# Attention stage of a hybrid trunk: two lanes of blocks become three, the lane table gets other numbers, and TensorE follows program order there

## The chip, the cores and the metric

The program runs on one core of a Trainium2 chip. The metric is the device time of one execution in microseconds. Three executions of the kernel before took 3175.34, 3176.96 and 3179.81 us; the median is 3176.96 us.

## The reference

Two layers of an encoder trunk over 1024 positions of width 1024, in float32. Layer 0 mixes with a recurrent part; layer 1, where the change is, mixes with chunked softmax attention over 16 heads of 64. Cut to what matters:

```python
def chunk_band_attention(h, w_qkv, q_g, k_g, rel_bias):
    qkv = (h @ w_qkv).reshape(bsz, seq, 3, C_HEADS, C_HEAD_DIM)
    q = rmsnorm(qkv[:, :, 0], q_g) * (C_HEAD_DIM ** -0.5)
    k = rmsnorm(qkv[:, :, 1], k_g)
    v = qkv[:, :, 2]
    ...
    bias = rel_bias[:, jnp.clip(rel, -C_MAX_REL, C_MAX_REL) + C_MAX_REL]
    def one_chunk(c):                       # 64 queries, own chunk and the 8 before
        s = jnp.einsum('bqhd,bkhd->bhqk', q_c, k_b) + bias
        prob = jax.nn.softmax(jnp.where(valid, s, -jnp.inf), -1)
        return jnp.einsum('bhqk,bkhd->bqhd', prob, v_b)
```

After it come the output projection, a squared-ReLU MLP and a gated embedding, as in layer 0.

## The kernel before

The attention part of layer 1 is written as generators ("lanes") that a small planner, `run` (L128), steps through. The planner has a clock of its own, `now`. Each product that a lane emits adds its estimated TensorE time. When a lane yields a name, it may go on only once the number under that name in the table `LAT` has passed; when it yields a tuple such as `("at", 3)`, it sleeps until another lane marks that tuple. Among the lanes that may go on, the first in the list is taken. So the table and the list decide the order in which instructions are written.

Work is cut into 16 steps `s`: head pair `pr` and half `hf` of the sequence. Three kinds of lane run:

- `attn_ins` (last in the list) makes queries, keys and values of a step. Each step has four chunks of 128 rows, and a chunk is 24 matmuls of 384 columns into a bank named `dps` (two banks). ScalarE and VectorE read each chunk out (L1742, L1746, L1747), GpSimd squares the result in two halves (`sq`, L1754), and VectorE sums and normalises. This lane may be three steps ahead of the attention, no more (`("at", s - 3)`). After step 15 it goes on with dense products of the tail (`dps<-act,wq`, 512 columns).
- `attn_norms` transposes the queries and keys of a step on TensorE (`dps<-ident,qk`) and splits them into a high and a low part (`F`, `Ql`).
- `attn_lane` (two of them before) takes the next of 64 blocks: a step, one of its two heads, and two row tiles of 128 queries. For each of the two tiles a block computes the near scores into `sn` (two banks), adds the bias `toep` and takes the maximum on VectorE (L1838); computes the far scores, where there are any, into `sf` (one bank; L1845 to L1848 read it); and takes exponentials, sum and scale on ScalarE and VectorE (L1848 to L1855) in a tile `pb`. Then it transposes `pb` on TensorE into `pt` (two banks, L190), splits that into `ptile` on ScalarE and VectorE (L347, L348), and multiplies with the values into `po` (one bank). Half 1 of a pair has far scores in all its tiles, half 0 only in its last one.

The names that the planner looks up in a block are `attn_block0` (after each tile's scores), `attn_block1` (between the scores and the transposes), `attn_block2` (after each bank of transposes) and `attn_block3` (before the product with the values).

What is written is not what an engine runs. The framework schedules each engine's queue anew by its own timeline model, so before the change TensorE's order in this stage is the framework's, not the lanes'. Each engine then runs its queue strictly in that order, waiting on semaphores.

Of the kernel before, what the change touches and what calls it, by code (L numbers as in the profile page):

```python
# [17 lines left out]
P = 128  # L18
# [3 lines left out]
HB = 512  # L22
NT = T // P
C = 128
NEG = -1.0e30
# [54 lines left out]
    "gdn_back2": 0.48,  # L80
    "gdn_back3": 1.30,
    "gdn_back4": 1.83,
    "attn_norm0": 0.24,
    "attn_block0": 0.97,
    "attn_block1": 4.45,
    "attn_block2": 0.43,
    "attn_block3": 0.94,
    "qk": 11.25,
    "norm": 1.28,
    "end_front": 46.33,  # L90
    "end_mid": 0.83,
    "end_back": 1.12,
# [15 lines left out]
class Trunk:  # L108
# [1510 lines left out]
    def layer1_in(self):  # L1619
        nc, tc, a = self.nc, self.tc, self.a  # L1620
        with ExitStack() as es:
            self.psm = es.enter_context(self.pool("psml1", space=PSUM))
            wp = self.wp = es.enter_context(self.pool("l1a", 2))
            self.wr = es.enter_context(self.pool("l1wr", 2))
            self.w1 = es.enter_context(self.pool("l1w1"))
            l1 = es.enter_context(self.pool("l1", 2))
            self.sm = es.enter_context(self.pool("sml1", 2))
            self.yd = [[self.dr.tile([P, HB], F32, tag=f"yd{k}{hf}", name="yd") for hf in range(2)] for k in range(NK)]
            rbl = l1.tile([P, 16], F32, tag="rbl", name="rbl", bufs=1)
            nc.sync.dma_start(out=rbl, in_=a["rb_last"].rearrange("(o c) -> o c", o=1).broadcast_to((P, 16)))  # L1630
# [45 lines left out]
    def attn_norms(self, steps, l1):  # L1676
# [11 lines left out]
    def attn_lane(self, steps, jobs, l1, rbl):  # L1688

        for s, h, b in jobs:  # L1690
            yield ("in", s)
            yield from self.attn_block(s, *steps[s], h, b, l1, rbl)

    def weights3(self, odd):

# [89 lines left out]
            st[nm] = F  # L1785
            yield "attn_norm0"

    def attn_block(self, s, pr, hf, h, blk, l1, rbl):

        nc, psm, sm = self.nc, self.psm, self.sm  # L1790
        V, A, G = nc.vector, nc.scalar, nc.gpsimd
        st = self.st[s]
        m0 = 4 * hf + 2 * blk
        if hf == 0 and blk == 0:
            t = st["toep"][h]
            G.tensor_scalar(t, t, rbl[:, 2 * pr + h:2 * pr + h + 1], None, op0=ALU.subtract)
# [31 lines left out]
        for m in (m0, m0 + 1):  # L1828
            n0 = max(0, m - 2)
            nn = m - n0 + 1  # L1830
            f0 = max(0, m - 4)
            nf = n0 - f0
            pn = psm.tile([P, HB], F32, tag="sn", name="sn", bufs=2)
            score(pn[:, 0:nn * P], m, n0, nn)
            mx = sm.tile([P, 4], F32, tag="mx", name="mx", bufs=4)
            pb = self.wp.tile([P, 5 * P], F32, tag="pb", name="pb", bufs=4)
            S = pb[:, nf * P:(nf + nn) * P]
            V.tensor_tensor_reduce(S, pn[:, 0:nn * P], toep[:, (3 - nn) * P:], op0=ALU.add, op1=ALU.max,  # L1838
                                   scale=1.0, scalar=NEG, accum_out=mx[:, 0:1])
            l = sm.tile([P, 4], F32, tag="l", name="l", bufs=4)  # L1840
            if nf:
                pf = psm.tile([P, HB], F32, tag="sf", name="sf")
                score(pf[:, 0:nf * P], m, f0, nf)
                if m >= 4:
                    V.memset(pf[64:128, 0:64], NEG)  # L1845
                V.reduce_max(mx[:, 1:2], pf[:, 0:nf * P], axis=AX.X)
                V.tensor_scalar(mx[:, 2:3], mx[:, 0:1], mx[:, 1:2], -1.0, op0=ALU.max, op1=ALU.mult)
                A.activation(pb[:, 0:nf * P], pf[:, 0:nf * P], AF.Exp, bias=mx[:, 2:3], accum_out=l[:, 1:2])  # L1848
            else:
                V.tensor_scalar(mx[:, 2:3], mx[:, 0:1], -1.0, None, op0=ALU.mult)  # L1850
            A.activation(S, S, AF.Exp, bias=mx[:, 2:3], accum_out=l[:, 0:1])
            if nf:
                V.tensor_tensor(l[:, 0:1], l[:, 0:1], l[:, 1:2], op=ALU.add)
            V.reciprocal(l[:, 2:3], l[:, 0:1])
            A.activation(pb[:, 0:(nf + nn) * P], pb[:, 0:(nf + nn) * P], AF.Copy, scale=l[:, 2:3])  # L1855
            probs.append((pb, f0))
            yield "attn_block0"
# [9 lines left out]
        for b in range(bank + 1):  # L1867
            pt = psm.tile([P, HB], F32, tag="pt", name="pt", bufs=2)
            for j, (bb, o, c0, c1) in place.items():
                if bb != b:  # L1870
                    continue
                for e in range(2):
                    if c0 <= 128 * e < c1:
                        pb, f0 = probs[e]
                        self.tr(pt[:, o + 128 * e - c0:o + 128 * e - c0 + P],
                                            pb[:, (j - f0) * P:(j - f0 + 1) * P], self.ident)
            t = self.wp.tile([P, 2, HB], F32R, tag="ptile", name="ptile", bufs=3)
            self.split_scaled(t, pt[:, 0:used[b]], None, slice(0, used[b]))
            pts.append(t)
            yield "attn_block2"  # L1880
# [3 lines left out]
        for j, c0, c1 in segs:  # L1884
            b, o, _, _ = place[j]
# [112 lines left out]
```

## Time and profile before

| what | value |
|---|---|
| median of three runs | 3176.96 us |
| the profiled execution, its own time | 3175.69 us |
| span of the profiled execution | 3174.0 us |
| mean granted TensorE clock over the span | 0.973 |
| first dense product of the attention stage starts | 1751.1 us |
| first scores start | 1789.4 us |
| last product with the values ends | about 2371 us |

The profile counts time from the first instruction. Rows of a listing in order of time begin with start and duration; rows of groups give line, engine, operation, output and inputs, count, then busy time and mean duration, then the time that the engine sat idle just before these instructions and what ended that wait. "PE" is TensorE's matrix array, "PEld" its weight load, DVE is VectorE, ACT is ScalarE, POOL is GpSimd, SPq the queue that issues most transfers. A matmul's recorded duration includes its run through the array, and the next may start before it ends, so a matmul's duration is longer than the distance between two starts. The attention stage is the stretch from 1751 to 2371 us. Layer 0 lies before it; the dense products of the tail lie behind it.

### The profile page before, as it was taken

The page shows a single profiled execution, that of the slowest core. Times are in us where ns is not written, and L with a number is a line of the kernel's source. Part 1 is how long each engine was busy: PE and PEld are TensorE (multiplying, and loading weights), DVE is VectorE, ACT ScalarE, POOL GpSimd, SP SyncE. Part 2 cuts the span into 40 slices and gives each one's busy share as a digit, 9 for nine tenths or more (in the row PEclk, how much of TensorE's full clock was granted, in tenths as well). Part 3 has the DMA queues.
Part 4 walks back from the last instruction along what each step waited for, and adds up shares of the span by engine and source line. Part 5 has one row for each costly group of instructions (what it writes and reads, how often), then busy time and mean ns, then how long its engine had stood idle before and what let it go on. Part 6 is the DMA issues. An engine that isn't in the chain of part 4 may idle for free.

```text
span 3174.0 us, 46034 instructions
## 1 busy us (share of the span) xinstructions
PE 3057.5 (96%) x17576; PEld 2523.9 (80%) x17576; DVE 2018.1 (64%) x4020; ACT 1387.8 (44%) x2640; POOL 536.1 (17%) x978
## 2 busy tenths in 40 slices
PE   7999999999999999999999989999999999999999
PEld 5777777777778888888887888888788888888887
DVE  6546666567849666655556576776769666655552
ACT  4323433333427554311223577777757555312221
POOL 6524443444500000000005111110200000000002
PEclk8989999999999999999999999999999999999999
DMA  3212112112345333522213100110255332522213
GB/s 128 77 48 64 50 43 85 54 57 64 126 153 209 136 120 112 190 93 100 99 54 129 58 32 33 47 39 16 76 197 205 136 120 107 199 93 93 107 47 106
DMA packets 144716, 309.60 MB, mean 98 GB/s; under 512 B 40944, under 2 KB 43120, under 8 KB 144496
## 3 DMA queue, kind: packets, MB, share of 16 engines
q1 hardware_dynamic: 126064, 273.10, 25.1%
q10 hardware_dynamic: 18432, 33.56, 2.7%
q8 instruction: 138, 2.26, 0.3%
q14 instruction: 82, 0.67, 0.1%
HBM read 232.16 MB, written 74.45 MB: 97 GB/s over the span
## 4 chain that ended last, share of the span: by engine, by line
PE 79%; DVE 10%; ACT 4%; DMA 4%; issue 2%; POOL 1%; SPq 0%; DVEq 0%; POOLq 0%; ACTq 0%
PE dps L175 67%; PE ch L175 2%; PE po L175 1%; PE pm L175 1%; PE iz L175 1%; PE tp L175 1%; DVE ptile L348 1%; PE pt L190 1%; DVE f L1056 1%; DMA wraw<-in_w_out 1%; PE sn L175 1%; DMA wraw<-in_w_qkv 1%; DVE wlo L302 1%; DVE pb L1838 1%; POOL subt L413 1%
## 5 line engine op out<-in xcount | busy, mean ns | idle before, releaser
L175 PE MATMUL dps<-r,act 128*128 128x512 f32 x3528 | 824.4, 392 | 0.0
L175 PEld LDWEIGHTS dps<-r,act 128*128 128x128 f32 x3528 | 662.2, 188 | 145.6
L175 PE MATMUL dps<-xg,whi 128*128 128x512 f32 x1280 | 437.9, 423 | 16.2 <-ACT xg L350 7.1
L175 PE MATMUL dps<-late,act 128*128 128x512 f32 x1536 | 352.9, 391 | 0.0
L175 PEld LDWEIGHTS dps<-late,act 128*128 128x128 f32 x1536 | 288.5, 188 | 63.1
L1495 POOL TENSOR_TENSOR pn<-pn,prs 128x512 f32<-128x512 f32 x32 | 47.1, 1475 | 1621.3 <-ACT prs L384 1527.3
L175 PE MATMUL dps<-wq,act 128*128 128x384 f32 x1536 | 304.8, 343 | 8.0 <-DVE vs L1747 4.2
L175 PEld LDWEIGHTS dps<-xg,whi 128*128 128x128 f32 x1280 | 237.2, 197 | 67.0 <-ACT xg L350 7.1
L175 PEld LDWEIGHTS dps<-wq,act 128*128 128x128 f32 x1536 | 264.5, 190 | 12.6 <-DVE vs L1747 7.0
L175 PE MATMUL dps<-xg,wlo 128*128 128x512 f32 x640 | 260.4, 408 | 2.0 <-DVE wlo L302 2.0
L1371 DVE TENSOR_TENSOR late<-late,dps 128x512 f32<-128x512 f32 x224 | 152.7, 684 | 152.4 <-PE dps L175 120.3
L1470 DVE TENSOR_TENSOR xw<-xw,dps 128x512 f32<-128x512 f32 x192 | 131.5, 685 | 154.6 <-PE dps L175 151.4
L1269 ACT CAST act<-act 128x1024 fp32r<-128x1024 f32 (+1 forms) x99 | 94.7, 963 | 282.9 <-DMA act<-in_w 119.4
L1269 ACT CAST act<-late 128x512 fp32r<-128x512 f32 x210 | 124.5, 618 | 139.5 <-PE dps L175 120.2
L1270 DVE TENSOR_TENSOR act<-late,act 128x512 fp32r<-128x512 f32 x210 | 139.7, 686 | 25.9 <-ACT act L1269 25.7
L175 PEld LDWEIGHTS dps<-xg,wlo 128*128 128x128 f32 x640 | 125.5, 196 | 33.2 <-DVE wlo L302 4.1
L301 ACT CAST whi<-wraw 128x1024 fp32r<-128x1024 f32 x78 | 81.7, 1048 | 152.7 <-PE dps L175 91.4
L175 PE MATMUL dps<-xw,act 128*128 128x512 f32 x576 | 138.9, 392 | 0.0
L175 PEld LDWEIGHTS dps<-xw,act 128*128 128x128 f32 x576 | 108.1, 188 | 24.1
L1270 DVE TENSOR_TENSOR act<-act 128x1024 fp32r<-128x1024 f32 (+1 forms) x99 | 109.9, 1114 | 18.3 <-ACT act L1269 17.2
L175 PE MATMUL po<-ptile,vs 128*128 128x256 f32 (+1 forms) x576 | 103.3, 293 | 17.5 <-DVE ptile L348 8.5
L302 DVE TENSOR_TENSOR wlo<-wraw,whi 128x1024 fp32r<-128x1024 f32 x78 | 99.3, 1274 | 27.5 <-ACT whi L301 27.1
(472 smaller groups left out, 5284.9 us busy)
## 6 DMA issues: line engine op xcount, KB each, us to landing
act<-in_w SPq DMA_DIRECT2D x68, 512.0 KB
hd<-late ACTq DMA_DIRECT2D x128, 256.0 KB
late<-in_w SPq DMA_DIRECT2D x60, 512.0 KB
wraw<-in_w_in SPq DMA_DIRECT2D x56, 512.0 KB
act<-hd SPq DMA_DIRECT2D x56, 512.0 KB
wraw<-in_w_out SPq DMA_DIRECT2D x21, 512.0 KB
wraw<-in_w_qkv SPq DMA_DIRECT2D x21, 512.0 KB
pn<-pnd SPq DMA_DIRECT2D x32, 256.0 KB
```

Of the source, the lines that this page charges most:

```text
L175: return self.begin(self.nc.tensor.matmul(out, lhsT, rhs, start=start, stop=stop))
L190: return self.begin(self.nc.tensor.transpose(out, in_, ident))
L301: nc.scalar.copy(hi, raw)
L302: nc.vector.tensor_tensor(lo, raw, hi.bitcast(F32), op=ALU.subtract)
L348: nc.vector.tensor_tensor(dst[:, 1, sl], src, dst[:, 0, sl].bitcast(F32), op=ALU.subtract)
L413: E.tensor_tensor(o, X[:, 0:i, i:i + 1].broadcast_to((NP, i, n)), Bq[:, i:i + 1, i + 1:16].broadcast_to((NP, i, n)), op=ALU.mult)
L1056: V.scalar_tensor_tensor(y, raws[j][:, i:i + HB], cw(i), y, op0=ALU.mult, op1=ALU.add)
L1269: A.copy(hi, s)
L1270: V.tensor_tensor(lo, s, hi.bitcast(F32), op=ALU.subtract)
L1371: V.tensor_tensor(r, t, u, op=ALU.add)
L1470: V.tensor_tensor(x[n][:, sl], x[n][:, sl], ps, op=ALU.add)
L1495: G.tensor_tensor(pn, pn, prs[:, sl], op=ALU.mult)
```

## The change

Three things change in this stage, and nothing elsewhere.

1. Seven numbers of the table `LAT` become larger. The planner's waits inside a block and before a step's scores grow with them.
2. Three `attn_lane` generators run where two did. Two tiles get more buffers to match: `pb` 6 for 4, `ptile` 4 for 3. The banks `sn`, `sf`, `pt`, `po` and `dps` stay as many as they were.
3. The lanes run inside a context that keeps TensorE in program order; the other engines are scheduled by the framework as before.

The subtraction that prepares the bias tile (two GpSimd instructions per head) also moves: from the first block of each head into `attn_norms`, for both heads at once.

```diff
-    "attn_block0": 0.97,
-    "attn_block1": 4.45,
+    "attn_block0": 1.80,
+    "attn_block1": 7.00,
...
-            self.run([self.attn_lane(steps, jobs, l1, rbl) for _ in range(2)] + [self.attn_norms(steps, l1), self.attn_ins(steps, l1)])
+
+            with tc.manual_schedule(engines={mybir.EngineType.PE}):
+                self.run([self.attn_lane(steps, jobs, l1) for _ in range(3)] + [self.attn_norms(steps, l1, rbl), self.attn_ins(steps, l1)])
...
+            for h in range(0 if hf else 2):
+                t = self.st[s]["toep"][h]
+                self.nc.gpsimd.tensor_scalar(t, t, rbl[:, s + h:s + h + 1], None, op0=ALU.subtract)
+                self.nc.gpsimd.memset(t[0:64, 320:384], NEG)
...
-        if hf == 0 and blk == 0:
-            t = st["toep"][h]
-            G.tensor_scalar(t, t, rbl[:, 2 * pr + h:2 * pr + h + 1], None, op0=ALU.subtract)
-            G.memset(t[0:64, 320:384], NEG)
...
-            pb = self.wp.tile([P, 5 * P], F32, tag="pb", name="pb", bufs=4)
+            pb = self.wp.tile([P, 5 * P], F32, tag="pb", name="pb", bufs=6)
...
-            t = self.wp.tile([P, 2, HB], F32R, tag="ptile", name="ptile", bufs=3)
+            t = self.wp.tile([P, 2, HB], F32R, tag="ptile", name="ptile", bufs=4)
```

TensorE runs the same instructions in both kernels. How they stand differs over the whole stage; three places follow. A row is one or more instructions next to each other in an engine's queue, with line, operation, output and inputs, shape, count, and in brackets the engines whose semaphores the first of them waits for.

**First place, TensorE, the far scores of step 3** (second half of the second head pair). Before, ahead of the step's second group of far scores (`sf`):

```order
L175 MATMUL po<-ptile,vs 128x256 [waits Activation_49]
L175 MATMUL po<-ptile,vs 128x256 [waits DVE_49]
L175 MATMUL po<-ptile,vs 128x128 x2
L175 MATMUL dps<-wq_16732,act 128x384
L175 MATMUL dps<-wq_16733,act 128x384
L175 MATMUL dps<-wq_16732,act 128x384 x2
L175 MATMUL dps<-wq_16733,act 128x384
L175 MATMUL dps<-wq_16732,act 128x384
L175 MATMUL sf<-F_16433,F_16928 128x256 [waits Activation_49]
L175 MATMUL sf<-F_16433,Ql 128x256
```

After, from the step's first scores on:

```order
L175 MATMUL sn<-F_16322,F_16920 128x256 [waits Activation_49]
L175 MATMUL sn<-F_16322,Ql 128x256
L175 MATMUL sn<-F_16892,F_16920 128x128
L175 MATMUL sn<-F_16892,Ql 128x128
L175 MATMUL sf<-F_16322,F_16920 128x256
L175 MATMUL sf<-F_16322,Ql 128x256
L175 MATMUL sn<-F_16892,F_16920 128x384
L175 MATMUL sn<-F_16892,Ql 128x384
L175 MATMUL sf<-F_16322,F_16920 128x256 [waits Activation_49]
L175 MATMUL sf<-F_16322,Ql 128x256
L190 MATMUL pt<-ident,pb 128x128 x4
```

Before, 30 dense matmuls and other work stand between the first and the second group of far scores of this step; now two matmuls do, and the second group waits for ScalarE to have read the only `sf` bank.

**Second place, TensorE, a block's product with the values** (`po`), in the same region. Before:

```order
L175 MATMUL po<-ptile,vs 128x256 [waits Activation_49]
L175 MATMUL po<-ptile,vs 128x256 [waits DVE_49]
L175 MATMUL po<-ptile,vs 128x256 x2
L175 MATMUL po<-ptile,vs 128x256 [waits Activation_49]
L190 MATMUL pt<-ident,pb 128x128 [waits PE_49]
L190 MATMUL pt<-ident,pb 128x128 x2
L175 MATMUL po<-ptile,vs 128x256 [waits DVE_49]
L175 MATMUL po<-ptile,vs 128x128 x2
```

After:

```order
L175 MATMUL dps<-wq_16747,act 128x384 x2
L175 MATMUL dps<-wq_16748,act 128x384
L175 MATMUL dps<-wq_16747,act 128x384
L175 MATMUL po<-ptile,vs 128x256 x4
L175 MATMUL po<-ptile,vs 128x256 [waits Activation_49]
L175 MATMUL po<-ptile,vs 128x256 [waits DVE_49]
L175 MATMUL po<-ptile,vs 128x128 x2
```

Before, products with the values and transposes of the next block alternate, a few of each; now a block's transposes stand first, dense matmuls behind them (15 here, the last rows of them shown), and the products with the values in one run behind those.

**Third place, GpSimd, the preparation of a bias tile** (`toep`) beside the squares (`sq`) of a later step. Before:

```order
L1754 TENSOR_TENSOR sq<-qk 128x512 [waits DVE_49,Activation_49] x2
L1796 TENSOR_SCALAR toep<-toep,rbl 128x384 [waits DMAHW1_49,DVE_49]
L1797 MEMSET toep 64x64 [waits Pool_49]
L1754 TENSOR_TENSOR sq<-qk 128x512 [waits Activation_49]
L1754 TENSOR_TENSOR sq<-qk 128x512 [waits DVE_49,Activation_49]
```

After:

```order
L1760 TENSOR_TENSOR sq<-qk 128x512 [waits DVE_49,Activation_49]
L1686 TENSOR_SCALAR toep<-toep,rbl 128x384 [waits DMAHW1_49,DVE_49]
L1687 MEMSET toep 64x64 [waits Pool_49]
L1760 TENSOR_TENSOR sq<-qk 128x512 [waits Activation_49]
L1760 TENSOR_TENSOR sq<-qk 128x512 [waits DVE_49,Activation_49]
```

The preparation, which waits for a transfer, stood between the squares of two steps; here it stands between the two halves of one step's squares.

More of the change, by code (lines that the diff above doesn't have):

```diff
@@ L82 @@
     "gdn_back4": 1.83,
-    "attn_norm0": 0.24,
-    "attn_block0": 0.97,
-    "attn_block1": 4.45,
[L86 to L89, printed above, removed]
+    "attn_norm0": 0.60,
+    "attn_block0": 1.80,
+    "attn_block1": 7.00,
+    "attn_block2": 0.60,
+    "attn_block3": 2.60,
+    "qk": 18.00,
+    "norm": 3.00,
     "end_front": 46.33,
@@ L1674, in attn_ins, with attn_norms @@
                                   [("at", 14), ("at", 14), ("at", 14), ("at", 15)])
-    def attn_norms(self, steps, l1):
+    def attn_norms(self, steps, l1, rbl):
         K = []
@@ L1686, in attn_norms, with attn_lane @@
             self.mark(("in", s), self.lat["norm"])
-    def attn_lane(self, steps, jobs, l1, rbl):
+    def attn_lane(self, steps, jobs, l1):
         for s, h, b in jobs:
             yield ("in", s)
-            yield from self.attn_block(s, *steps[s], h, b, l1, rbl)
+            yield from self.attn_block(s, *steps[s], h, b, l1)
     def weights3(self, odd):
@@ L1786, in attn_norm, with attn_block @@
             yield "attn_norm0"
-    def attn_block(self, s, pr, hf, h, blk, l1, rbl):
+    def attn_block(self, s, pr, hf, h, blk, l1):
         nc, psm, sm = self.nc, self.psm, self.sm
```

## The prediction

> **What bounds the kernel now.** I read the page first, then the stretches of the stage, then single groups.
>
> ```profile
> span 3174.0 us, 46034 instructions
> ...
> PE 3057.5 (96%) x17576; PEld 2523.9 (80%) x17576; DVE 2018.1 (64%) x4020; ACT 1387.8 (44%) x2640; POOL 536.1 (17%) x978
> ```
>
> TensorE is busy almost everywhere, so what the change is worth must be read inside its own stage:
>
> ```profile
> core 0: us, PE busy (x) PEld busy (x) DVE busy (x) ACT busy (x) POOL busy (x), PEclk, DMA share, GB/s
> 1751.00:1789.00 38.00, 36.33 (x198) 35.63 (x199) 15.71 (x42) 11.29 (x23) 5.93 (x7) 0.94 0.15 49
> 1789.00:2371.00 582.00, 535.64 (x3311) 493.40 (x3311) 414.62 (x1316) 422.55 (x985) 69.63 (x68) 0.98 0.17 59
> ```
>
> In 582 us with blocks TensorE is idle for 46.4, and 1.7 in the 38 us before: 48 in all. VectorE and ScalarE are busy 415 and 423, so TensorE bounds the stage, with two engines not far behind. But the idle time understates what could be saved, since a matmul counts as busy while it only runs through the array. I therefore count the work by distances between starts.
>
> ```profile
> 1761.76 0.47 ACT L1742 ACTIVATE qk<-dps,rscol 128x256 f32<-128x256 f32 x1 [3.54 <-PE dps L175]
> 1765.92 0.47 ACT L1742 ACTIVATE qk<-dps,rscol 128x256 f32<-128x256 f32 x1 [3.43 <-PE dps L175]
> 2008.81 0.60 PE L190 MATMUL dps<-ident,qk 128*128 128x128 f32 x4
> ```
>
> A chunk of 24 dense matmuls is read out every 4.16 us: 0.173 us for 384 columns, 0.451 ns a column. By the column that makes 0.231 us for 512, 0.115 for 256, 0.058 for 128. Four transposes take 0.60 us, the last of them 0.277 (below), so 0.108 each.
>
> ```profile
> L175 PE MATMUL dps<-wq,act 128*128 128x384 f32 x1512 | 299.9, 343 | 7.0 <-DVE vs L1747 4.2 <-DVE F L1783 1.9 <-DVE ms L373 0.8
> L190 PE MATMUL pt<-ident,pb 128*128 128x128 f32 x480 | 85.9, 285 | 10.9 <-ACT pb L1855 7.0 <-DVE ptile L348 3.6
> L175 PE MATMUL po<-ptile,vs 128*128 128x256 f32 x384 | 76.4, 311 | 17.3 <-DVE ptile L348 8.5 <-ACT ptile L347 7.7 <-DVE l L1853 0.3
> L175 PE MATMUL dps<-act,wq 128*128 128x512 f32 x283 | 75.9, 409 | 2.7 <-ACT act L1554 0.8 <-DVE Ql L1783 0.8 <-ACT wq L1658 0.8
> L175 PE MATMUL po<-ptile,vs 128*128 128x128 f32 x192 | 33.5, 258 | 0.1
> L190 PE MATMUL dps<-ident,qk 128*128 128x128 f32 x128 | 19.9, 277 | 2.6 <-DVE vs L1747 2.4
> ```
> ```profile
> L175 PE MATMUL sn<-F,Ql x160: 218/283/387, 1789.9 to 2327.3; 128*128 128x384 f32 x64, 128*128 128x128 f32 x48, 128*128 128x256 f32 x48
> L175 PE MATMUL sf<-F,Ql x96: 222/278/416, 1790.2 to 2346.2; 128*128 128x128 f32 x48, 128*128 128x256 f32 x48
> ```
>
> The dense group has 1536 matmuls on the code (64 chunks of 24; some records are missing): 266 us. Transposes: 608 x 0.108 = 66. Products with the values: 384 x 0.115 + 192 x 0.058 = 55. Dense work of the tail: 283 x 0.231 = 65. Scores: each of the last two rows has a twin of the same shapes for the high part, so 128 x 0.173 + 192 x 0.115 + 192 x 0.058 = 55. Together 507 of the 620 us from 1751 to 2371. **About 113 us are lost**: 48 named as idle, 65 hidden in short gaps.
>
> [...]
>
> **The change part by part.** The work on TensorE stays; nothing outside the stage moves. So the sum is over what the new order does to these 113 us. In the order of both kernels I measured, between the instruction that fills a buffer and the one that needs it, how much TensorE work stands, with the distances above. Where it is less than the other engines need, TensorE waits.
>
> *Products with the values.* They wait for `ptile`:
>
> ```profile
> L190 PE MATMUL pt<-ident,pb x480: 270/273/476, 1798.4 to 2365.1; 128*128 128x128 f32 x160
> L347 ACT CAST ptile<-pt x144: 351/577/611, 1800.6 to 2365.4; 128x512 fp32r<-128x512 f32 x80, 128x384 fp32r<-128x384 f32 x32, 128x256 fp32r<-128x256 f32 x32
> L348 DVE TENSOR_TENSOR ptile<-pt,ptile x144: 403/672/693, 1801.1 to 2365.8; 128x512 fp32r<-128x512 f32 x80, 128x384 fp32r<-128x384 f32 x32, 128x256 fp32r<-128x256 f32 x32
> ```
>
> 0.27 + 0.58 + 0.67 is 1.5 us, with hand-overs some 1.6. Of 144 such places 63 have less than that before, short by 43.5 us in all; after, 28, short by 16.0. The shortfalls add up to more than the idle time, because one wait covers the next, so I take only their ratio: of 17.4 us idle 37% stays. **Gain 11** (0 to 17).
>
> *Transposes into `pt`.* Its two banks come free by the same steps. Places under 1.6 us: 34 before, short by 18.5; after 8, short by 5.2. Of 10.9 us idle 28% stays: **gain 8** (0 to 11).
>
> *Dense products and near scores.* Their idle time is 7.0 + 2.7 + 2.6 in the rows above. VectorE's queue agrees with TensorE's now: before, 75 of its 128 reads of near scores stand behind something that TensorE does over 0.5 us of work later, after, none. **Gain 3** (0 to 8).
>
> *Short gaps.* 65 us. TensorE's instructions that carry a wait fall from 740 to 455, 61%. If gaps fell alike, 25 us would go; but a wait that is already satisfied need not cost anything, so nothing is the other end. **Gain 14**, between the ends, as part of these gaps is the pipeline tail of the long waits that go.
>
> *Far scores.* Little time is lost for them before:
>
> ```profile
> L175 PE MATMUL sf<-F,F 128*128 128x256 f32 x48 | 16.0, 334 | 1.5 <-ACT pb L1848 1.5
> L175 PE MATMUL sf<-F,F 128*128 128x128 f32 x48 | 12.5, 277 | 3.0 <-ACT pb L1848 2.5
> ```
>
> Here the order is worse: one bank, and the lanes that wake together when a step's keys are ready write their far scores close to each other (first place of the order).
>
> ```profile
> L1845 DVE MEMSET sf<- x64: 112/112/112, 1809.5 to 2349.2; 64x64 f32 x64
> L1846 DVE TENSOR_REDUCE mx<-sf x80: 284/414/425, 1791.7 to 2351.0; 128x1 f32<-128x256 f32 x64, 128x1 f32<-128x128 f32 x16
> L1847 DVE TENSOR_SCALAR mx<-mx 128x1 f32<-128x1 f32 x80 | 16.6, 208 | 1.2
> L1848 ACT ACTIVATE pb<-sf,mx x80: 345/474/507, 1795.3 to 2352.3; 128x256 f32<-128x256 f32 x64, 128x128 f32<-128x128 f32 x16
> ```
> ```profile
> L1848 ACT ACTIVATION_READ_ACCUMULATOR pb<-sf,mx 128x1 f32 x80 | 15.8, 198 | 0.0
> L1851 ACT ACTIVATE pb<-pb,mx 128x384 f32<-128x384 f32 x96 | 58.6, 610 | 4.1 <-DVE mx L1850 4.0
> L1851 ACT ACTIVATION_READ_ACCUMULATOR pb<-pb,mx 128x1 f32 x128 | 24.6, 192 | 0.0
> L1855 ACT ACTIVATE pb<-pb,l 128x640 f32<-128x640 f32 x64 | 53.2, 832 | 12.6 <-DVE l L1854 10.7 <-DVE ss L1756 1.6
> L1854 DVE RECIPROCAL l<-l 128x1 f32<-128x1 f32 x128 | 20.2, 159 | 8.9 <-ACT pb L1851 6.8
> L1853 DVE TENSOR_TENSOR l<-l 128x1 f32<-128x1 f32 x80 | 13.4, 167 | 28.2 <-ACT pb L1851 27.7
> ```
>
> A bank comes free no sooner than 0.28 + 0.11 + 0.41 + 0.21 + 0.47 = 1.5 us after its last matmul. When several follow each other, ScalarE sets the pace: exponentials, sums read back and scale are 0.47 + 0.20 + 0.61 + 0.19 + 0.83 = 2.3 us a tile, and between them it waits for sum and reciprocal on VectorE, 0.33: 2.6. Of 79 places 11 are below 2.6 us before, short by 12.1; after, 37, short by 34.7. With one bank these gaps don't overlap, so I take the difference whole: **loss 23**. At 1.5 us it would be 11.1 against 2.5, a loss of 9; at 3.0, where VectorE and ScalarE serve other lanes in between, 51.1 against 16.8, a loss of 34; beyond that, 43 for waits that queue up, worked out below.
>
> *The bias tile.* GpSimd, 70 us busy in 582, does the same 16 preparations. Placed between two halves of a step's squares, one holds back the second half, and VectorE's sum behind it:
>
> ```profile
> 2027.04 0.33 SPq L1722 DMA_DIRECT2D toep<-in_rb  x1
> 2029.64 2.32 POOL L1796 TENSOR_SCALAR toep<-toep,rbl 128x384 f32<-128x384 f32 x1 [7.96 <-DVE y L1897]
> ```
>
> In 6 of the 16 places the transfer (2.6 us from issue to the step's start here) and the step itself have less work to hide under, by 1 to 2 us each. What needs the sum is the next step's transposes, a dozen chunks away; I take **0**, with 6 lost at the other end. Larger buffers for `pb` and `ptile` move nothing through the engines; their gain is in the shortfalls above.
>
> The sum, against the profiled execution's own 3175.69 us (1.27 under the median): 11 + 8 + 3 + 14 - 23 = 13 us gained, **3163 us**.
>
> **The rivals.**
>
> *Slower.* The far scores cost more than the 36 us that the other terms bring; that is the point from which it decides. Walking through the first place in order with the rows above, the second, third and fourth `sf` of step 3 wait 2.4, 1.2 and 3.4 us: 7 us, where the count at 2.6 us gives 6. The third value grows because VectorE reads the sum of one tile ahead of the scores of the next. Such runs open the far scores of nearly all eight second halves; the first is the longest, seven in a row. Eight at 7, less the 13 that it costs before, is a loss of 43, and there is the clock:
>
> ```profile
> 1880.00:1920.00 40.00, 37.15 (x243) 36.24 (x242) 29.33 (x94) 28.75 (x67) 5.99 (x7) 0.96 0.06 21
> 2280.00:2320.00 40.00, 36.35 (x187) 30.99 (x186) 33.18 (x96) 31.93 (x72) 13.30 (x10) 0.87 0.46 157
> ```
>
> TensorE is granted 0.96 and 0.87 where it has much idle time, 1.6 and 5.2 us lost in 40. The waits of a run are split by other work, so I take the cheaper row: eight new runs at 1.6 are 13 us more. 36 - 43 - 13 is 20 slower: **3196**. For it: `sf` is the one bank that three lanes share. Against: waits there let the other engines catch up, so later waits shrink.
>
> [...]
>
> *No change.* The short gaps stay (they belong to the instructions, not to their order), and the far scores take the other 22: 22 - 23 leaves about **3176**. For it: VectorE and ScalarE at 71 and 73% of the stage leave little room to serve earlier. Against: the two terms rest on different rows.
>
> *A large gain.* Far scores cost 9, the waits go entirely (17 + 11 + 8) and the gaps fall with their count (25): 52, **3124**. For it: three lanes give each block more time from scores to transposes (the middle of 128 places grows from 8.4 to 12.2 us of work). Against: it needs every term at its end.
>
> That TensorE's order isn't kept is excluded by the order of the built program.
>
> **How the numbers follow.** The forecast (a gain of 7 to 35) has 0.45, the large gain 0.07, no change 0.24, slower 0.24. A measurement of this kernel can tell about 0.2%, 6 us. So faster 0.52, same 0.24, slower 0.24. The range runs from the large gain to the slower case, leaving out a little beyond each: 3126 to 3194.
>
> **What would show it.** In the changed profile: idle time of TensorE before `po` down from 17 to about 7 and before `pt` from 11 to 3 (else terms one and two are wrong); before `sf` up from 4.5 to some 25, released by ScalarE's exponential; the stage 10 to 15 us shorter from first dense product to last `po`, corrected for tail work that moved behind it; the granted clock in the stage still about 0.98. The prediction is wrong if TensorE's waits for `sf` pass 36 us, or if VectorE waits for GpSimd at the squares by more than a microsecond each time.

## The result, and the profile after

The changed kernel takes 3293.29 us (median), the kernel before 3178.39 on the same chip: ratio 1.0365, 95% interval 1.0341 to 1.039. One of the four executions of the kernel before took 3767.58 us, a slow run that the ratio leaves out; the median of the other three is 3176.96. The changed kernel is slower by 115 us, far outside the range, and on the side of the rival that was priced at 20 us.

The page of the changed kernel, its own time 3291.2 us, opens with the span and the busy times:

```profile
span 3289.5 us, 46044 instructions
...
PE 3093.0 (94%) x17576; PEld 2560.7 (78%) x17576; DVE 2028.4 (62%) x4020; ACT 1395.3 (42%) x2640; POOL 533.9 (16%) x978
```

TensorE runs the same 17576 matmuls, and the other engines have hardly more to do. The view by stretches for the same 548 us of the stage, before first and after behind it:

```profile
core 0 of [0], span 3174.0 us
core 0: us, PE busy (x) PEld busy (x) DVE busy (x) ACT busy (x) POOL busy (x), PEclk, DMA share, GB/s
1751.00:2299.00 548.00, 502.71 (x3157) 470.52 (x3158) 382.57 (x1247) 392.16 (x927) 69.10 (x71) 0.98 0.12 42
```
```profile
core 0 of [0], span 3289.5 us
core 0: us, PE busy (x) PEld busy (x) DVE busy (x) ACT busy (x) POOL busy (x), PEclk, DMA share, GB/s
1751.00:2299.00 548.00, 456.91 (x2676) 434.71 (x2675) 325.57 (x1056) 335.55 (x787) 46.08 (x54) 0.89 0.09 30
```

In equal time TensorE gets through 2676 matmuls where it did 3157, and VectorE, ScalarE and GpSimd are less busy too: no other engine became the bound, they all wait more. Two things went wrong at once. Idle time of TensorE rose from 45 to 91 us, and the granted clock fell from 0.98 to 0.89; the clock's missing share times 548 us is 11 us before and 60 after. The last product with the values ends at 2461 us where it ended at 2371.

Where the idle time stands, in the groups of TensorE by shape (changed kernel):

```profile
L175 PE MATMUL dps<-wq,act 128*128 128x384 f32 x1511 | 327.8, 367 | 20.0 <-DVE vs L1753 15.7 <-DVE Ql L1789 4.2
L190 PE MATMUL dps<-ident,qk 128*128 128x128 f32 x128 | 22.0, 300 | 27.1 <-DVE F L1789 24.3 <-ACT sq L1554 2.0 <-DVE vs L1753 0.8
L175 PE MATMUL dps<-act,wq 128*128 128x512 f32 x336 | 91.7, 421 | 6.3 <-ACT sq L1554 2.4 <-ACT act L347 1.6 <-DVE F L1789 1.3
L175 PE MATMUL sf<-F,F 128*128 128x256 f32 x48 | 17.6, 366 | 21.1 <-ACT pb L1850 21.0
L175 PE MATMUL sf<-F,F 128*128 128x128 f32 x48 | 12.2, 270 | 8.1 <-ACT pb L1850 8.1
L190 PE MATMUL pt<-ident,pb 128*128 128x128 f32 x480 | 83.6, 295 | 16.8 <-DVE ptile L348 11.9 <-DVE mx L1852 4.9
L175 PE MATMUL po<-ptile,vs 128*128 128x256 f32 x384 | 63.0, 300 | 9.8 <-DVE ptile L348 5.1 <-ACT ptile L347 4.7
L175 PE MATMUL po<-ptile,vs 128*128 128x128 f32 x192 | 33.6, 284 | 4.2 <-DVE ptile L348 2.7 <-ACT ptile L347 1.4
```

Far scores cost 29.2 us, about what was forecast. But the products with the values gained only 3 us, the transposes into `pt` lost 6, and the largest new wait stands where the prediction had only a small gain: 27.1 us before the transposes of queries and keys, and 20.0 before the dense products, which together had 9.6. They share the two `dps` banks.

The order of the built programs shows why. TensorE's rows about the transposes of a step's keys (first `ident,qk`) and queries (second); before:

```
L190 MATMUL dps<-ident,qk 128x128 x4
L175 MATMUL dps<-wq_17549,act 128x384
L175 MATMUL po<-ptile,vs 128x256 x2
L175 MATMUL po<-ptile,vs 128x128 x2
L190 MATMUL pt<-ident,pb 128x128 x2
L175 MATMUL dps<-wq_17548,act 128x384 x2
L190 MATMUL pt<-ident,pb 128x128 x5
L175 MATMUL dps<-wq_17549,act 128x384
L175 MATMUL dps<-wq_17548,act 128x384
L175 MATMUL po<-ptile,vs 128x256 x5
L190 MATMUL pt<-ident,pb 128x128 x3
L190 MATMUL dps<-ident,qk 128x128 x4
```

and in the changed kernel:

```
L190 MATMUL dps<-ident,qk 128x128 x4
L175 MATMUL sn<-F_17333,F_17353 128x384
L175 MATMUL sn<-F_17333,Ql 128x384
L175 MATMUL sf<-F_17333,F_17353 128x128
L175 MATMUL sf<-F_17333,Ql 128x128
L175 MATMUL dps<-wq_17555,act 128x384
L175 MATMUL dps<-wq_17556,act 128x384
L175 MATMUL dps<-wq_17555,act 128x384
L190 MATMUL dps<-ident,qk 128x128 x4
L175 MATMUL dps<-wq_17555,act 128x384
```

Before, the five dense matmuls between the two groups end the chunk, so the queries can take its bank. In the changed kernel three stand there and the chunk goes on behind: it holds one bank, and the queries must take the bank of the keys, which is read out a median 3.6 us after its last transpose. In 13 of the 16 steps the queries now meet an open chunk; before, in none. One such place in order of time, TensorE alone, with the wait that ended in brackets:

```profile
2053.55 0.60 PE L190 MATMUL dps<-ident,qk 128*128 128x128 f32 x4
...
2054.51 0.73 PE L175 MATMUL dps<-wq,act 128*128 128x384 f32 x3
2057.92 1.09 PE L190 MATMUL dps<-ident,qk 128*128 128x128 f32 x4 [2.68 <-DVE F L1789]
2058.66 2.27 PE L175 MATMUL dps<-wq,act 128*128 128x384 f32 x6
2062.14 1.31 PE L175 MATMUL dps<-wq,act 128*128 128x384 f32 x6 [1.21 <-DVE vs L1753]
```

The clock in the same place, by stretches of 3.4 us:

```profile
2050.90:2054.30 3.40, 3.40 (x26) 3.33 (x26) 1.53 (x6) 1.74 (x5) 0.00 (x0) 1.00 0.01 2
2054.30:2057.70 3.40, 0.94 (x7) 0.62 (x5) 2.83 (x7) 2.39 (x6) 0.00 (x0) 1.00 0.00 0
2057.70:2061.10 3.40, 3.01 (x10) 2.53 (x10) 0.92 (x4) 2.48 (x6) 0.00 (x0) 0.50 0.00 0
2061.10:2064.50 3.40, 2.36 (x18) 2.36 (x18) 2.02 (x4) 2.11 (x5) 1.04 (x1) 1.00 0.00 0
```

TensorE works for 0.94 us of one stretch, and in the next it is granted half clock: 6 dense matmuls take 2.27 us, against 1.31 for 6 at 2062.14, at full clock. So the wait of 2.68 us is paid for once more behind it.

Behind 1751 us, the start of the stage, both kernels run some 7000 matmuls, the same ones but for a few at the boundary; before first, after behind it:

```profile
1751.00:3174.00 1423.00, 1369.86 (x7000) 1182.16 (x7000) 909.24 (x2013) 720.75 (x1441) 97.23 (x91) 0.99 0.27 95
1751.00:3289.50 1538.50, 1412.01 (x6999) 1223.65 (x6997) 917.43 (x2008) 727.56 (x1441) 93.10 (x90) 0.95 0.25 87
```

TensorE's idle time grew there from 53 to 126 us and its busy time from 1370 to 1412, though the work is the same: 73 and 42 us make the 115.

### The profile page after: what moved, and what is told of

Same layout as the page of the kernel before. It is cut to its first block, busy times and chain, and to the rows that moved or that the text cites. A ratio compares the mean times of both kernels' runs of the same rounds, so it can differ in the third digit from the quotient of the medians.

```text
span 3289.5 us, 46044 instructions
## 1 busy us (share of the span) xinstructions
PE 3093.0 (94%) x17576; PEld 2560.7 (78%) x17576; DVE 2028.4 (62%) x4020; ACT 1395.3 (42%) x2640; POOL 533.9 (16%) x978
## 4 chain that ended last, share of the span: by engine, by line
PE 78%; DVE 9%; ACT 4%; DMA 4%; POOL 2%; issue 2%; SPq 0%; ACTq 0%; DVEq 0%; POOLq 0%
PE dps L175 66%; PE ch L175 2%; PE po L175 2%; PE pt L190 1%; PE pm L175 1%; PE iz L175 1%; PE tp L175 1%; PE sn L175 1%; POOL subt L413 1%; DVE f L1056 1%; POOL sub L415 1%; PE sf L175 1%; DVE wlo L302 1%; DVE pb L1840 1%; ACT F L1786 1%
## 5 line engine op out<-in xcount | busy, mean ns | idle before, releaser
L175 PE MATMUL dps<-wq,act 128*128 128x384 f32 x1536 | 333.2, 367 | 21.1 <-DVE vs L1753 15.7
L175 PEld LDWEIGHTS dps<-wq,act 128*128 128x128 f32 x1536 | 288.5, 207 | 26.1 <-DVE vs L1753 16.3
L1371 DVE TENSOR_TENSOR late<-late,dps 128x512 f32<-128x512 f32 x224 | 153.0, 685 | 152.8 <-PE dps L175 121.8
L1375 ACT ACTIVATE late<-late 128x512 f32<-128x512 f32 x128 | 80.2, 629 | 84.4 <-DVE late L1371 80.2
```

The costliest lines, as they stand in the source:

```text
L175: return self.begin(self.nc.tensor.matmul(out, lhsT, rhs, start=start, stop=stop))
L1371: V.tensor_tensor(r, t, u, op=ALU.add)
L1375: A.activation(t, t, AF.Relu)
```

## The experiments

Theory **P**: keeping TensorE in program order costs the time. Its rivals: **L** and **B**, the third lane with the larger waits, or the moved bias preparation, cost it whatever the order; **T**, the new numbers of the table are the damage under program order.

### Which part of the change

e1_no_order takes the context away and leaves the rest of the change:

```diff
-            with tc.manual_schedule(engines={mybir.EngineType.PE}):
-                self.run([self.attn_lane(steps, jobs, l1) for _ in range(3)] + [self.attn_norms(steps, l1, rbl), self.attn_ins(steps, l1)])
+            self.run([self.attn_lane(steps, jobs, l1) for _ in range(3)] + [self.attn_norms(steps, l1, rbl), self.attn_ins(steps, l1)])
```

> The changed kernel with TensorE's order given back to the framework; three lanes, the new table, the larger buffers and the moved bias preparation stay. The changed kernel takes 3293 us, the kernel before 3178. Theory P (program order on TensorE is what costs: it makes TensorE stand at a wait while other work that is ready lies behind it): 3160 to 3195, TensorE's idle time in the stage back to about 50 us from 124, clock in the stage back to 0.97 or more. Rival L (the third lane and the larger waits bunch the blocks, whatever the order): stays above 3240. Rival B (the bias preparation, moved on GpSimd, holds back the squares): stays above 3240 too, with GpSimd's wait for the bias transfer still near 122 us.

e2_order_only puts that context around the two lanes of the kernel before:

```diff
-            self.run([self.attn_lane(steps, jobs, l1, rbl) for _ in range(2)] + [self.attn_norms(steps, l1), self.attn_ins(steps, l1)])
+            with tc.manual_schedule(engines={mybir.EngineType.PE}):
+                self.run([self.attn_lane(steps, jobs, l1, rbl) for _ in range(2)] + [self.attn_norms(steps, l1), self.attn_ins(steps, l1)])
```

> The kernel before with one thing added: TensorE keeps program order in the attention stage. Two lanes, old table, old buffers. Theory P: most of the loss is there alone, 3230 or more, and with the short old waits perhaps more than the changed kernel's 3293, since the table decides how much dense work stands between a buffer's writer and its reader. Rival L: within 0.5% of the kernel before, 3165 to 3195.

e3_order_times is e2 with the seven new numbers of the table, e4_old_times the changed kernel with the seven old ones.

> The kernel before with program order on TensorE and the new table, still two lanes and the old buffers. Theory P with the one scores bank and the dense banks as the places of the waits: between 3230 and 3300; two lanes send fewer far scores at once, so the idle time before the far scores is less than the 29 us of the changed kernel, and that before the transposes of queries and keys is the same 27 us. Rival L (third lane): 3180 to 3210.

> The changed kernel with the old seven numbers in the table; three lanes and program order on TensorE stay. Theory P: 3300 or more, because the old waits put less work between writer and reader; idle time before the products with the values and before the transposes of the probabilities rises above 14 and 17 us. Rival T (the new numbers are the damage, as they let blocks gather): 3180 to 3220.

| kernel | order | lanes | table | us | against before (interval) |
|---|---|---|---|---|---|
| e1_no_order | framework | 3 | new | 3188.02 | 1.0032 (1.002 to 1.0043) |
| e2_order_only | program | 2 | old | 3255.21 | 1.025 (1.0225 to 1.0275) |
| e3_order_times | program | 2 | new | 3340.65 | 1.0514 (1.0493 to 1.0534) |
| e4_old_times | program | 3 | old | 3348.23 | 1.053 (1.0501 to 1.0558) |
| changed kernel | program | 3 | new | 3293.29 | 1.0365 (1.0341 to 1.039) |

P holds, L, B and T fall: without program order the third lane, the table, the buffers and the bias preparation together cost 0.3%, about 10 us; with it every combination is slower by 2.5 to 5.3%. The size depends on lanes and table together: with three lanes the old numbers are worse than the new, with two lanes it is the other way round. In e1 TensorE's clock over the same 548 us is 0.97 again. My sizes missed: e3 came out above its range, and e4 for another reason than expected. Its idle time before the products with the values (11.2 us) and the transposes of the probabilities (4.1) did not rise. It stood at the far scores and at the transposes of queries and keys (e4_old_times, TensorE by shape):

```profile
L175 PE MATMUL sf<-F,F 128*128 128x128 f32 x48 | 15.4, 328 | 23.2 <-ACT pb L1850 23.2
L175 PE MATMUL sf<-F,F 128*128 128x256 f32 x48 | 22.4, 466 | 36.2 <-ACT pb L1850 36.2
L190 PE MATMUL dps<-ident,qk 128*128 128x128 f32 x128 | 22.6, 306 | 39.2 <-DVE F L1789 37.4 <-DVE qk L1764 1.7
L190 PE MATMUL pt<-ident,pb 128*128 128x128 f32 x480 | 78.6, 279 | 4.1 <-DVE ptile L348 3.2 <-DVE l L1856 0.7
```

These two places are in all four kernels with program order: 29, 29, 30 and 59 us at `sf`, 27, 34, 42 and 39 at the queries and keys (changed kernel, e2, e3, e4). Hence theory **D**: program order costs what it costs because it meets single banks that must be emptied by slower engines. Its rivals: **M**, the waits only move when one bank is given more room, and **C**, the half clock has another cause.

### Which banks

In e5, e6, e7 and e11 and later in e15, TensorE's rows in the stage stand in the same order as in the changed kernel; only the banks differ that they write. (The framework orders the other engines, so theirs can differ.)

e5_qk_in_pt writes the transposed queries and keys into the two `pt` banks:

```diff
-            pt = self.bank()
+            pt = self.psm.tile([P, HB], F32, tag="pt", name="pt", bufs=2)
```

> The changed kernel (3293 us) with the transposed queries and keys written into the two pt banks instead of the two dps banks, so that the dense chunk, which keeps one dps bank while it is half done, no longer leaves a single bank to both. Theory D (that single bank is a main place of the loss: 27.1 us idle before these transposes and 20.0 before the dense products): those two fall below 15 together, the time to between 3235 and 3260, more than the idle time that goes, because the half clock falls too (157 us of it in the stage now). Rival M (the waits only move: the pt banks come free as late, 16.8 us idle there now): idle before pt rises by 25 or more, time 3280 to 3300.

Measured 3264.13 us, 29 less. The dense products' 20.0 us went (the group is below 1 us); the queries and keys kept 16.7 of their 27.1, now behind `ptile`, and the other groups took some of the rest (e5_qk_in_pt):

```profile
L190 PE MATMUL pt<-ident,qk 128*128 128x128 f32 x128 | 19.8, 279 | 16.7 <-DVE ptile L348 11.7 <-DVE F L1789 5.0
L190 PE MATMUL pt<-ident,pb 128*128 128x128 f32 x480 | 84.0, 295 | 25.9 <-DVE ptile L348 10.7 <-DVE F L1789 5.5 <-DVE Ql L1789 4.5
L175 PE MATMUL sf<-F,F 128*128 128x256 f32 x48 | 18.1, 377 | 27.9 <-ACT pb L1850 27.9
```

So D in part and M in part: the time is just outside the range of D, the two places of D still have 17 us where it said below 15, and the idle time at `pt` rose by 26, as M said. The half clock in the stage (every stretch at half clock that lies in it wholly or partly) fell from 157 us to 126 with these waits, which speaks against C; the last section has more on it.

e6_two_sf puts two far scores into the two halves of their bank by turns; e7_both is e5 and e6 together; e8_no_order_sf is e6 without program order.

```diff
+            self.sfs, self.nsf = self.psm.tile([P, 2, 256], F32, tag="sf", name="sf"), 0
...
-                pf = psm.tile([P, HB], F32, tag="sf", name="sf")
+                self.nsf = 1 - self.nsf
+                pf = self.sfs[:, self.nsf]
```

> The changed kernel with the far scores in the two halves of their one bank by turns (a far score has 256 columns at most, the bank holds 512), so that two can be on their way. The order on TensorE stays. Theory D: idle time before sf falls from 29.2 to below 10 and the time to between 3250 and 3265. Rival M (ScalarE's exponentials set the pace, so a second place only moves the wait to the near scores or to the transposes): sf falls but sn, pt or po rise by as much, 3280 to 3300.

> Both of the edits before in one kernel, program order kept. Theory D: the two gains add, 3190 to 3225, and the half clock in the stage falls from 157 us to below 90. If half clock is set by something other than these waits (rival C), idle time falls by 60 us but the half clock stays above 130 and the time above 3230. Rival M: above 3270.

> The changed kernel without program order (3188 us here) with the two places for far scores. Under the framework's order idle time before sf is 3 to 5 us in all, so both theories give little: 3180 to 3190. If it falls below 3175, the framework's model of the order was itself held by the one bank.

They took 3294.46, 3258.71 and 3190.05 us: the halves change nothing, not even the wait they were meant for (30.9 us at `sf` in e6). A far score still started 0.14 us behind the exponential of the one before, 28 times against 26 in the changed kernel. So the edit gave no second place, and neither D nor M is tested by it. The trace does not show whether the wait stands there because both halves lie in one bank or because they are one tile.

e11_ring gives the scores real banks, one ring of three for near and far in place of two and one, on top of e5. e9_sf_gap instead leaves the banks as in the changed kernel and makes the planner wait until 2.6 us of planned work lie between two far scores.

```diff
-            pn = psm.tile([P, HB], F32, tag="sn", name="sn", bufs=2)
+            pn = psm.tile([P, HB], F32, tag="s", name="sn", bufs=3)
...
-                pf = psm.tile([P, HB], F32, tag="sf", name="sf")
+                pf = psm.tile([P, HB], F32, tag="s", name="sf", bufs=3)
```
```diff
+    def hold(self, tag, n, t):
+        q = self.held.setdefault(tag, [])
+        while len(q) >= n and self.now < q[-n] + t:
+            yield "gap"
+        q.append(self.now)
...
+                yield from self.hold("sf", 1, 2.6)
                 pf = psm.tile([P, HB], F32, tag="sf", name="sf")
```

> The kernel with queries and keys transposed in pt (3264 us), with near and far scores taking three banks in turn, in place of two for the near and one for the far scores; the order on TensorE is the same. This does what the two halves of one bank did not do: there each far score still started 0.14 us behind the exponential of the one before, so the halves were still treated as one. Theory D: idle time before sf (36 us) and sn together falls below 15, the time to 3225 to 3245. Rival M: the idle time goes to pt and po, 3255 or more.

> The changed kernel with one rule more in the planner: a far score may be written only 2.6 us of planned TensorE work after the one before it, so that other work stands between two users of the one sf bank. Program order on TensorE stays. Theory D (waits at single banks make the loss): idle time before sf falls from 29 to about 10 (places with less than 2.6 us of work in between fall from 37 to 11), the time to 3250 to 3270. Rival M (the wait only moves): 3280 to 3300. Rival S (the shortfall of order is not what sets these waits, but how late VectorE and ScalarE answer): sf stays above 20.

e11 took 3221.67 us, 42 less than e5 and a little below the range of D, with the same order of TensorE. The wait at `sf` went and did not come back elsewhere in full (e11_ring):

```profile
L175 PE MATMUL sf<-F,F 128*128 128x256 f32 x48 | 15.5, 322 | 5.2 <-DVE mx L1840 4.9 <-ACT pb L1850 0.2
L175 PE MATMUL sf<-F,F 128*128 128x128 f32 x48 | 11.7, 259 | 1.2 <-ACT pb L1850 1.2
L190 PE MATMUL pt<-ident,qk 128*128 128x128 f32 x128 | 20.4, 285 | 16.9 <-DVE ptile L348 13.1 <-DVE F L1789 3.8
L190 PE MATMUL pt<-ident,pb 128*128 128x128 f32 x480 | 81.2, 288 | 29.5 <-DVE ptile L348 16.5 <-DVE F L1789 5.4 <-DVE mx L1852 4.4
```

e9 took 3275.36, between the ranges of D and M: the wait at `sf` fell to 18.2 us only, where D had about 10, and the one at the queries and keys rose to 37.1. Spacing by a table of planned times is worth less than a bank.

e12_all_gaps and e13_ring_gaps add the same rule for `pt` (2.0 us from the last use but one) to e5, with the rule for `sf` in e12 and with the ring in e13.

> Queries and keys in pt, the rule of 2.6 us for sf, and the same rule for the two pt banks (2.0 us from the last but one use). Theory D: idle time before sf below 12, before pt below 25 (43 without the rules), 3210 to 3240. Rival M: above 3255.

> Queries and keys in pt, the ring of three banks for all scores, and the rule of 2.0 us for pt. Theory D: the best with program order, 3200 to 3230; half clock in the stage below 90 us (157 in the changed kernel). Rival M: above 3250.

They took 3236.01 and 3220.5. The first lies in its range, but its idle time missed by far: 22.8 us at `sf` and 54.8 at `pt` (40.1 and 14.7), where 12 and 25 were expected. The second is no better than e11 without the rule, and its half clock is 92 us, where below 90 was expected. The rule brings nothing that a ring does not.

### All banks in one ring

Some 43 us over the kernel before were left in e11, with 46 us of idle time at `pt`. e15_ring5 makes one ring of the five banks that scores, transposed probabilities and transposed queries and keys use (`sn` 2, `sf` 1, `pt` 2; no bank more than before). e16_no_order_ring5 is that without program order, e17_before_ring5 the kernel before with the same ring, e18_before_ring3 the kernel before with the ring of three for the scores alone.

```diff
-            pn = psm.tile([P, HB], F32, tag="sn", name="sn", bufs=2)
+            pn = psm.tile([P, HB], F32, tag="s", name="sn", bufs=5)
...
-                pf = psm.tile([P, HB], F32, tag="sf", name="sf")
+                pf = psm.tile([P, HB], F32, tag="s", name="sf", bufs=5)
...
-            pt = psm.tile([P, HB], F32, tag="pt", name="pt", bufs=2)
+            pt = psm.tile([P, HB], F32, tag="s", name="pt", bufs=5)
...
-            pt = self.bank()
+            pt = self.psm.tile([P, HB], F32, tag="s", name="pt", bufs=5)
```

> The changed kernel, program order kept, with one ring of five banks for near scores, far scores, transposed probabilities and transposed queries and keys; dps and po keep theirs. Theory D (the rest of the loss is waits for single banks, now pt): idle time before pt falls from 46 us to below 20, the time to 3175 to 3205. Rival O (program order costs something beyond its waits for banks: work that is ready stands behind a product that waits for ScalarE or VectorE): idle time before pt and po stays 40 or more, 3210 to 3240.

> The same with TensorE's order left to the framework (3188 us with the old banks). Theory D: 3170 to 3190, within 20 us of the kernel with program order and the same banks. Rival O: 3160 to 3185, and 30 or more below the one with program order.

> The kernel before with the ring of five banks, two lanes, the old table, the framework's order. Idle time before pt is 10.9 there and before sf 4.5, so by the waits at most 15 us could go: 3165 to 3180. More than 3185 would say that one ring makes a score wait for a transpose that has nothing to do with it.

> The kernel before with the ring of three banks for the scores alone. Idle time before sf is 4.5 us and before sn below 1: 3172 to 3180. In the changed kernel the same edit gave 42 us, so a difference below 6 here says that the one sf bank is a bottleneck of program order, not of the kernel.

| kernel | us | against before (interval) |
|---|---|---|
| e15_ring5, program order | 3181.73 | 1.0018 (1.0002 to 1.0035) |
| e16_no_order_ring5 | 3132.07 | 0.9866 (0.9843 to 0.9889) |
| e17_before_ring5 | 3152.02 | 0.9924 (0.9906 to 0.9942) |
| e18_before_ring3 | 3146.06 | 0.9904 (0.9885 to 0.9923) |

The same order of TensorE that cost 3.65% with separate banks costs 0.2% with one ring: 112 us went with the banks, the waits for them and what those brought with them. That is not 112 of the price of program order alone, since the ring gives the kernel before 25 us as well (e17). `pt` is free now, but the products with the values wait more than in the changed kernel (e15_ring5):

```profile
L190 PE MATMUL pt<-ident,pb 128*128 128x128 f32 x480 | 81.1, 290 | 1.1 <-DVE mx L1840 1.1
L175 PE MATMUL po<-ptile,vs 128*128 128x256 f32 x384 | 66.5, 305 | 24.2 <-DVE ptile L348 11.7 <-ACT ptile L347 5.1 <-DVE ss L1762 2.9
```

In e15 itself rival O is not met: 25 us of idle time at `pt` and `po` where it said 40 or more, and 3182 us for at least 3210. Against the framework's order it is: with the same banks, that order is 50 us faster (e16), more than I gave it, and waits less at `po` (e16_no_order_ring5):

```profile
L175 PE MATMUL po<-ptile,vs 128*128 128x256 f32 x384 | 76.1, 297 | 6.2 <-DVE ptile L348 2.6 <-ACT ptile L347 2.0 <-DVE y L1898 1.2
```

The stretch of 548 us in e15 and in e16:

```profile
core 0 of [0], span 3178.1 us
core 0: us, PE busy (x) PEld busy (x) DVE busy (x) ACT busy (x) POOL busy (x), PEclk, DMA share, GB/s
1751.00:2299.00 548.00, 505.77 (x3179) 487.75 (x3178) 395.23 (x1269) 403.00 (x957) 68.60 (x72) 0.94 0.14 45
```
```profile
core 0 of [0], span 3127.5 us
core 0: us, PE busy (x) PEld busy (x) DVE busy (x) ACT busy (x) POOL busy (x), PEclk, DMA share, GB/s
1751.00:2299.00 548.00, 527.63 (x3418) 504.88 (x3417) 417.14 (x1340) 421.73 (x1002) 73.03 (x72) 0.99 0.18 59
```

e16 beats both kernels, the one before by 1.3% and the changed one by some 5%. Its three lanes and new table gain 20 us over e17, which has two lanes, the old table and the same ring: the intervals 0.9843 to 0.9889 and 0.9906 to 0.9942 do not meet. Over e18, the better of the two kernels with two lanes, it is 14 us, and there the intervals touch. With the old banks the same lanes and table lost 0.3% (e1). And the banks were a limit of the kernel before too, against my expectation: the ring of three alone gives it 30 us, though it waited only 4.5 at `sf`. These 30 us are not that wait (e18_before_ring3):

```profile
L175 PE MATMUL sf<-F,F 128*128 128x256 f32 x48 | 15.6, 325 | 6.1 <-DVE mx L1838 3.2 <-ACT pb L1848 2.8
L190 PE MATMUL pt<-ident,pb 128*128 128x128 f32 x480 | 78.3, 279 | 1.6 <-DVE ptile L348 1.4 <-ACT pb L1855 0.2
```

The wait at `sf` did not fall; the one at `pt`, whose banks are as before, fell from 10.9 to 1.6. Under the framework's order other banks bring another order of TensorE: the traces of e16, e17 and e18 show it changed over the whole stage. So the gains of these three are banks and order together, and no run parts them.

The price of separate banks is 112 us here under program order, where the order is the same (the changed kernel to e15). Without it the same ring is worth 56 us (e1 to e16), but with another order.

## Why the prediction was wrong, by its own steps

*The sign.* The forecast was 13 us gained; it is 115 lost. The step that failed is the one called "Dense products and near scores", gain 3. It took the rows 7.0, 2.7 and 2.6 us as the size of the matter and looked at VectorE's queue for near scores. The shared `dps` pair was not walked through in the new order, though the rows of before name its readers (`F`, `vs`). There stand 20.0, 6.3 and 27.1 us now, a loss of 41, because in 13 of 16 steps a half-done chunk holds one of the two banks. A small wait in the old profile is no bound on it in a new order.

*Products with the values*: to about 6.5 us, measured 14.0. *Transposes into `pt`*: to 3, measured 16.8. The order did improve as counted (8 places under 1.6 us for 34), the waits did not follow. One service time and a ratio of shortfalls stood in for a spread: from the last transpose of a bank to the end of its split it takes 2.0 us in the mean in the changed kernel, 2.5 or more for a quarter of them and 3.5 or more for a tenth. The spread is not new (before, 2.6 in the mean and 4.3 or more for a tenth); what is new is where it falls. At six reuses of a `pt` bank, five of them with about 1 us of work or less in between, the split took 3.6 to 4.4 us, and these six make some 16.7 us of waiting. Before, no reuse of a bank waited more than 0.8.

*Far scores*: loss 23, measured 24.7 (29.2 less 4.5). The mechanism and the size were right.

*Short gaps and the clock*: a gain of 14, with the clock "still about 0.98". Measured 0.89. Half clock in the stage grew from 34 to 157 us. This step failed too: the 42 us of busy time that TensorE needs more for the same work are lost here, by estimate all to the half clock, whose 123 us more can hold back up to 61 us of work. The other 73 of the 115 us are idle time, 68 of them at the places above. Fewer instructions with a wait did not help, since the waits left are long: distances between starts that are over 2 us too long went from 3 to 26.

*Bias tile*: 0, and that stands within some 10 us. GpSimd waits 121.8 us for the transfers instead of 47.6, and VectorE 7.9 us in all for the squares instead of 1.6, but without program order the same edit is in a kernel that loses 0.3% in all (e1, where GpSimd waits 76.6 for the transfers).

*The slower rival* had the right sign and one of the right places. Its price, 43 + 13, was short because it knew one bank of three, and a clock loss of 13 us where the missing clock grew by 49 in 548 us. Its 3196 is too low.

*The count of 113 us*: no records are missing from the dense group. Its first chunk, 24 matmuls, ran at 1735.6 us, ahead of the 1751 at which the stage is said to start. That makes 117 us lost in the stretch for 113. The 65 us called short gaps also hold the half clock of before, 28 us within the stretch, up to 14 us of it lost.

*Still open*: no run held the waits and took away the half clock, so what each would cost alone was not tried. Why the framework's order leaves less to wait for with equal banks, 50 us, is read from its waits (6.2 us before `po` against 24.2) and not tested further. Nor is it shown what of the 56, 25 and 30 us of e16, e17 and e18 is the banks and what the new order.

## What to carry to other kernels

When an order is fixed by hand, list every buffer that the engine writes, with its banks, and walk each through the new order with the time that its readers take, the ones that never waited first of all. Give one ring to tiles that come and go in turn before adding lanes: with five banks in one ring the third lane and its table gained 20 us, with the same banks split by use they lost 10 (both under the framework's order). Look at the longest waits and not at their sum alone: TensorE was idle for 42 of the 548 us in e15 and for 45 in the kernel before, but with 12 distances over 2 us too long in the stage for 3, and the granted clock in the 548 us was 0.94 for 0.98.

## What the runs showed of the hardware

In the traces of the two kernels the granted clock is full or half. In the stage (1751 us to the last product with the values) the kernel before has 6 stretches at half clock, 3.4 to 10.2 us long and 34 us in all, and the changed kernel 27, 3.4 to 23.9 us long and 157 us in all; the first of each begins before 1751 us. Ahead of the others TensorE had waited. In the 3.41 us just before them it sat idle for 1.8 to 2.1 us in the kernel before (five times, 1.95 in the mean), and for 1.3 to 3.2 us in the changed kernel (26 times, 2.14 in the mean). Not every such stretch was followed by half clock: from 1938.24 the changed kernel's TensorE was idle for 1.82 of 3.41 us, and the clock was 1.00 there and in the 3.41 us behind. Over the whole stage it is idle for 48 of 620 us and for 116 of 710, which is 0.26 and 0.56 us in 3.41.

In the kernel before, the longest single wait ahead of each of its five changes to half clock (a distance between starts beyond the columns' own time) was 2.0 to 2.2 us. The sum of idle time does not account for the clock in these runs: e15 has no more of it in the 548 us than the kernel before (42 and 45), but in its whole stage 12 distances that are over 2 us too long, where there were 3, and a clock of 0.94 for 0.98 over the 548 us; e16 has none, and 0.99.
